# One row in place of a broadcast load, and a pool closed in two steps: a transformer block on one core

## The chip, the cores and the metric

The kernel runs on one core of one Trainium2 chip. The core has five engines with queues of their own: TensorE (PE, matrix products), VectorE (DVE), ScalarE (ACT), GpSimd (POOL) and SyncE (SP), which here only issues the DMAs. Each engine takes its instructions strictly in the order in which the program has written them; engines wait for each other by semaphores. The metric is the device time of one execution in microseconds.

## The reference

One layer on 1024 tokens of width 1024, all in float32: a half-weighted SwiGLU feed-forward block, a mixing block with three kinds of attention, and a second feed-forward block like the first.

```python
def rms_norm(x, g):
    x32 = x.astype(jnp.float32)
    y = x32 * lax.rsqrt(jnp.mean(x32 * x32, axis=-1, keepdims=True) + EPS) * g.astype(jnp.float32)
    return y.astype(x.dtype)

def swiglu(h, w_in, w_out):
    gate, up = jnp.split(h @ w_in, 2, axis=-1)
    return (jax.nn.silu(gate) * up) @ w_out
...
    x = x + 0.5 * swiglu(rms_norm(x, ffn1_norm), ffn1_w_in, ffn1_w_out)
...
    x = x + mix @ w_mix_out
    x = x + 0.5 * swiglu(rms_norm(x, ffn2_norm), ffn2_w_in, ffn2_w_out)
```

D_FF is 2816, so `w_in` is 1024x5632 and `w_out` 2816x1024. `mix` is the sliding-window attention with sinks beside a gated sum of compressed, selected and windowed attention; the change doesn't touch it.

## The kernel before

**Numbers.** Every float32 operand of a product is split into a high part (`whi`, `gph`, names ending in h), which ACT or POOL makes by a copy, and a low part (`wlo`, `gpl`, names ending in l), which DVE makes by a subtraction. A product is three matmuls, high by high, high by low, low by high (`mm3`, lines 250 to 252).

**Stages.** A feed-forward block has two stages. The first (`first_stage`) computes gate and up. `X` (eight tiles x0 to x7 of 128 tokens) is normalised and flipped by PE transposes (`ntr`, line 312) into operands `A11`, `A12` (in `XN0`) and `A21`, `A22`, from which come further sums `S1` to `S4`. Columns n of `w_in` are then worked in groups of seven products, in which combinations of blocks stand for the eight of plain block multiplication; the last three products of a group take S3, S4 and A22 in this order (in the code m7, m3, m4). The results go to DRAM (`AS`). The second stage (`second_stage`) reads them back as `graw`, splits them into `gph` and `gpl`, and multiplies them with `w_out` (`wraw`, `whi`, `wlo`): steps k = 0 to 10 for each of seven products, twelve matmuls a step. The second block does the same with other names of pools.

**Pools.** The operands A21/S4 (one place for both), A22, S2, S1, S3 of the first stage lie in one pool `p_in` (line 573); at its end the pool is closed, and the second stage's pool `p_out` with `graw`, `gph`, `gpl` is opened over its place (`to_out`, `to_out2`). The kernel waits tile by tile for the users of the memory that a new tile lies over. Between the two, `p_xn` takes the place of S4 and A22 for the normalised rows of the next block.

**Order.** The order of every engine's instructions is made when the program is built. `Plan.run` keeps a list of tasks, each with an engine, a cost, a position, tasks that it depends on (`deps`), tasks that must have been written earlier (`after`) and slots of rings; it simulates the engines and writes the task that could begin first, by position among those that are near. So a task that becomes free earlier in the plan moves ahead in its engine's queue, and it holds whatever is behind it. The task `opened` carries `to_out`, and all second-stage loads have it in `after`:

```python
    opened = add(None, 0.0, at - 5.0, to_out, after=chain_[-1:])
```

`chain_` is the last seven products of the first stage, so `chain_[-1]` is m4 and `chain_[4]` is m7. A load of `graw` also depends on m6 (`chain_[2]`), its split on m7.

**Beginning.** `load_x` brings x0, `load_gain` the norm's vector with one DMA that reads the same 4 KB for each of the 128 partitions (512 KB arrive), then x1 and eight weight tiles of 256 KB (`wraw`) in turn with x2 to x7. `inv_rms` squares a tile in two halves on ACT (lines 500, 506), and finishes the reciprocal root in small DVE instructions (lines 473 to 476, 503, 509). `scale_in_place` (line 520) multiplies the tile with root and gain on DVE. POOL and DVE split the weights (lines 457, 460). PE fills its time with transposes of the identity (`warm`). `wraw` has four slots.

Of the kernel before, what the change touches and what calls it, by code (L numbers as in the profile page):

```python
# [8 lines left out]
F32 = mybir.dt.float32  # L9
F32R = mybir.dt.float32r  # L10
BF16 = mybir.dt.bfloat16
I32 = mybir.dt.int32
AF = mybir.ActivationFunctionType
# [8 lines left out]
KD = 8  # L22
# [35 lines left out]
class Units:  # L58
# [7 lines left out]
    def add(self, width, parts):  # L66
        self.units.append((width, parts))
        return len(self.units) - 1
# [120 lines left out]
def block_kernel(  # L189
# [26 lines left out]
    PE, ACT, DVE, POOL = nc.tensor, nc.scalar, nc.vector, nc.gpsimd  # L216
    ctx.enter_context(tc.manual_schedule())

    def pool(name, stack=None, **kw):
        return (stack or ctx).enter_context(tc.tile_pool(name=name, bufs=1, reuse_waits="tile", **kw))  # L220
# [84 lines left out]
    def load_gain(dst, g):  # L305
        dma(dst, dram_ap(g, 0, [[0, 128], [1, D]]))
# [17 lines left out]
    def xn_tiles(p):  # L324
        return [XA, [p.tile([128, KD, 512], F32R, name="xn1" + s) for s in "hl"]]
# [193 lines left out]
    def scale_in_place(t, r, gain, pos, deps):  # L519
        return add("D", 1.22, pos, lambda: DVE.scalar_tensor_tensor(  # L520
            X[t], X[t], r(), gain(), op0=OP.mult, op1=OP.mult), deps=deps)
# [39 lines left out]
    HALF = [slice(0, 512), slice(512, 1024)]  # L561
# [8 lines left out]
    def in_src(w_in, n, j, part):  # L570
        return dram_ap(w_in, 512 * j * 2 * FF + part * FF + n * 128, [[4 * 2 * FF, 128], [2 * FF, 4], [1, 128]])

    def open_in(p):

        t = {k: [p.tile([128, 4, 512], F32R, name=k + s) for s in "hl"] for k in ("S4", "A22", "S2", "S1", "S3")}
        t["A21"] = t["S4"]
        t["A11"], t["A12"] = XN0
        return t
# [357 lines left out]
    ph1 = ExitStack()  # L936
    nws = ExitStack()
    f_in = ExitStack()
    p_nw = pool("p_nwf", f_in, side="right")
    opn1 = open_in(pool("p_in", f_in))  # L940
    gain1 = p_nw.tile([128, D], F32, name="gain1")
    extra = [p_nw.tile([128, 512], F32, name="ext%d" % j) for j in range(2)]
    r_y = Ring("hr", [128, 4, 8], F32, 6)
    new_plan([])

    load_x(0, n=2)
    come = lambda at: add(None, 0.0, 0.0, lambda: None, tail=at)
    xt, raws1 = [[come(3.3), come(4.05)]] + [None] * 7, {}
    fetched[-1] = come(0.75)
    fetched.append(add("S", 1.46, -20.0, lambda: load_gain(gain1, ffn1_norm), after=fetched[-1:], tail=2.2))  # L950
    for w_ in (1, (0, 0, 0), (0, 0, 1), 2, (0, 1, 0), (0, 1, 1), 3, (1, 0, 0), (1, 0, 1), 4, (1, 1, 0), (1, 1, 1), 5, 6, 7):
        if type(w_) is tuple:
            raws1[w_] = fetch(in_src(ffn1_w_in, *w_), -20.0)
        else:
            fetched.append(add("S", 1.46, -20.0, lambda t=w_: load_x(t, n=2 if t < 4 else 1), after=fetched[-1:], tail=2.2))
            xt[w_] = [fetched[-1]]
    w_ = add(None, 0.0, 0.0, lambda: None, tail=1.4)
    for j in range(WARM):
        w_ = add("P", 0.64, 9.0, lambda: warm_up(3), deps=[w_], takes=[(r_mo, [])])
    scaled = {}  # L960
    for t in range(NT):
        p_ = 1.0 * t if t < 4 else 8.0 + 1.0 * t
        st, d, yu = inv_rms(t, p_, xt[t] if t == 0 else xt[t] * 2, True)
        scaled[t] = scale_in_place(t, lambda st=st: st["y"], lambda: gain1, p_, [d])
        yu.append(scaled[t])
    at, chain_, stored_, gone = first_stage(0, ffn1_w_in, ffn1_w_out, lambda: opn1, scaled, lambda: extra,
                                         lambda: [gain1[:, h] for h in HALF], 2.0, "G", [], 
                                              [(0, 256), (256, 512)], none, raws=raws1)

    def to_out():  # L970
        nonlocal p_nw, xn, p_o
        f_in.close()
        xn = xn_tiles(pool("p_xn", ph1))
        p_o = pool("p_out", f_out)
        p_nw = pool("p_nw", nws, side="right")
        mem["gain"] = p_nw.tile([128, D], F32, name="gainm")

    def parameters():
        load_gain(mem["gain"], mix_norm)
        for key, qn_, kn_ in (("a", q_norm_a, k_norm_a), ("b", q_norm_b, k_norm_b)):  # L980
# [1 line left out]
            gk[key] = p_o.tile([128, HD], F32, name="gk" + key)  # L982
            dma(gq[key], dram_ap(qn_, 0, [[0, 128], [1, HD]]))
            dma(gk[key], dram_ap(kn_, 0, [[0, 128], [1, HD]]))
    xn = p_o = None
    gq, gk = {}, {}
    f_out = ExitStack()
    opened = add(None, 0.0, at - 5.0, to_out, after=chain_[-1:])
    asked = add("S", 2.4, at + 14.0, parameters, deps=[add(None, 0.0, at, lambda: None, after=[opened], deps=chain_[-1:], tail=8.0)])
    r_nx = Slots(2)  # L990
    again = {t: [add("S", 1.46, at - 4.0 + t, lambda t=t: load_x(t), deps=gone, after=[opened], tail=2.2)]
             for t in range(NT)}
# [6 lines left out]
    at = second_stage(0, ffn1_w_out, at, opened, (chain_[2], chain_[4]), stored_, lambda: p_o, again, each)  # L999
# [963 lines left out]
        scaled[t] = scale_in_place(t, lambda t=t: R2[:, t:t + 1], lambda: nx["t"][:, 0, :D], p_, [put_, r_, gain2])  # L1963


    f_in, f_out = ExitStack(), ExitStack()
    opn2 = {"A11": XN0[0], "A12": XN0[1]}
    extra2 = []

    def to_ffn2():  # L1970
        att.close()
        kvs.close()
        opn2.update(open_in(pool("p_in2", f_in)))
        p = pool("p_nw2", f_in, side="right")
        extra2.extend(p.tile([128, 512], F32, name="ext2%d" % j) for j in range(4))
    settled = add(None, 0.0, tail + 10.0, to_ffn2, deps=attention, after=list(scaled.values()))
# [2 lines left out]

    def to_out2():  # L1980
        nonlocal p_o
        f_in.close()
        p_o = pool("p_out2", f_out)
    opened2 = add(None, 0.0, at - 5.0, to_out2, after=chain_[-1:])
    again = {t: [add("S", 1.46, at - 4.0 + t, lambda t=t: dma(X[t], XS[t]), deps=gone, after=[opened2], tail=2.2)]
             for t in range(NT)}
    xout = out.rearrange("b (t p) d -> (b t) p d", p=128)
# [3 lines left out]
    second_stage(1, ffn2_w_out, at, opened2, (chain_[2], chain_[4]), stored_, lambda: p_o, again, each2)  # L1991
    plan.run()
    f_out.close()


_INS = ['x', 'rel_bias_table', 'ffn1_norm', 'ffn1_w_in', 'ffn1_w_out', 'mix_norm', 'w_mix_in', 'w_mix_out',
# [26 lines left out]
```

## Time and profile before

| | us |
|---|---|
| median of 3 runs | 1943.32 |
| lowest, highest | 1943.04, 1943.46 |
| the profiled execution, its own time | 1940.19 |
| its span, first to last instruction | 1938.4 |
| PE busy in the span | 1892.4 (98%) |
| DVE, ACT, POOL busy | 1365.0, 917.4, 404.8 |

In the rows below the first number is a start in microseconds from the start of the span, the second a duration; "<-" stands between what an instruction writes and what it reads, xN for N instructions alike, and in brackets stands how long the engine had been idle before, and what ended that. Matmuls overlap, so the distance of two starts is their pace.

### The profile page before, as it was taken

The page shows a single profiled execution, that of the slowest core. Times are in us where ns is not written, and L with a number is a line of the kernel's source. Part 1 is how long each engine was busy: PE and PEld are TensorE (multiplying, and loading weights), DVE is VectorE, ACT ScalarE, POOL GpSimd, SP SyncE. Part 2 cuts the span into 40 slices and gives each one's busy share as a digit, 9 for nine tenths or more (in the row PEclk, how much of TensorE's full clock was granted, in tenths as well). Part 3 has the DMA queues.
Part 4 walks back from the last instruction along what each step waited for, and adds up shares of the span by engine and source line. Part 5 has one row for each costly group of instructions (what it writes and reads, how often), then busy time and mean ns, then how long its engine had stood idle before and what let it go on. Part 6 is the DMA issues. An engine that isn't in the chain of part 4 may idle for free.

```text
span 1938.4 us, 28044 instructions
## 1 busy us (share of the span) xinstructions
PE 1892.4 (98%) x9142; PEld 1580.0 (82%) x9142; DVE 1365.0 (70%) x3114; ACT 917.4 (47%) x1947; POOL 404.8 (21%) x544
## 2 busy tenths in 40 slices
PE   7999999999999999998899999989999999999999
PEld 6888888887888888887788788778888888878887
DVE  7687876665655677566888888876978766655553
ACT  5343333333444434245877888843433333344442
POOL 3011111111000112013754765530111111110000
PEclk9999999999999999998999999999999999999999
DMA  5277753336886337235202321022777533368662
GB/s 174 76 241 242 234 190 104 97 121 212 296 274 196 115 88 195 71 119 168 67 12 58 102 72 56 23 76 70 243 243 234 189 103 98 120 223 296 198 217 98
DMA packets 243955, 291.29 MB, mean 150 GB/s; under 512 B 24912, under 2 KB 138976, under 8 KB 243808
## 3 DMA queue, kind: packets, MB, share of 16 engines
q1 hardware_dynamic: 243808, 289.50, 46.3%
q8 instruction: 72, 1.18, 0.3%
q14 instruction: 75, 0.61, 0.1%
HBM read 202.24 MB, written 90.33 MB: 151 GB/s over the span
## 4 chain that ended last, share of the span: by engine, by line
PE 92%; DVE 3%; ACT 2%; POOL 1%; DMA 1%; issue 1%; SPq 0%; DVEq 0%; ACTq 0%; POOLq 0%
PE lg L250 13%; PE lg L252 13%; PE lg L251 13%; PE mo L250 6%; PE mo L252 6%; PE mo L251 6%; PE pv L250 4%; PE pv L252 4%; PE pv L251 4%; PE ptr L1825 3%; PE a L252 3%; PE a L251 3%; PE a L250 3%; PE pvo L1845 2%; PE pvo L1844 2%; PE lg L1650 2%
## 5 line engine op out<-in xcount | busy, mean ns | idle before, releaser
L801 POOL TENSOR_TENSOR x<-x,x 128x512 f32<-128x512 f32 x80 | 115.2, 1439 | 710.5 <-DVE x L797 670.0
L460 DVE TENSOR_TENSOR wlo<-wraw,whi 128x512 fp32r<-128x512 f32 x290 | 203.8, 708 | 74.9 <-ACT whi L455 70.8
L455 ACT ACTIVATE whi<-wraw 128x512 fp32r<-128x512 f32 x274 | 170.1, 623 | 111.3 <-PE lg L251 43.6
L460 DVE TENSOR_TENSOR gpl<-graw,gph 128x512 fp32r<-128x512 f32 x154 | 105.1, 689 | 142.7 <-ACT gph L455 142.6
L455 ACT ACTIVATE gph<-graw 128x512 fp32r<-128x512 f32 x154 | 96.1, 630 | 187.8 <-PE pv L251 84.7
L793 ACT ACTIVATE x<-lg 128x512 f32<-128x512 f32 x96 | 57.4, 598 | 157.7 <-PE lg L252 157.7
L1835 DVE TENSOR_TENSOR pl<-ptr,ph 128x512 fp32r<-128x512 f32 x178 | 116.5, 685 | 16.8 <-ACT ph L1833 15.5
L1833 ACT ACTIVATE ph<-ptr 128x512 fp32r<-128x512 f32 x178 | 98.7, 595 | 33.2 <-PE ptr L1825 31.8
L250 PE MATMUL a<-whi,gph 128*128 128x512 f32 x264 | 104.1, 394 | 3.6 <-ACT gph L455 3.6
L252 PE MATMUL a<-whi,gpl 128*128 128x512 f32 x264 | 104.0, 394 | 1.4 <-DVE gpl L460 1.4
L251 PE MATMUL a<-wlo,gph 128*128 128x512 f32 x264 | 103.6, 392 | 0.0
L88 POOL TENSOR_SCALAR whi<-wraw 128x512 fp32r<-128x512 f32 (+1 forms) x52 | 35.4, 685 | 325.3 <-PE mo L252 221.2
L250 PE MATMUL lg<-xn0h,whi 128*128 128x512 f32 (+1 forms) x264 | 100.5, 381 | 0.0
L251 PE MATMUL lg<-xn0l,whi 128*128 128x512 f32 (+1 forms) x264 | 99.9, 378 | 0.2 <-DVE xn0l L320 0.2
L252 PE MATMUL lg<-xn0h,wlo 128*128 128x512 f32 (+1 forms) x264 | 99.8, 378 | 0.0
L455 ACT ACTIVATE whi<-x 128x512 fp32r<-128x512 f32 x104 | 64.9, 628 | 72.5 <-PE lg L251 35.9
L460 DVE TENSOR_TENSOR wlo<-x,whi 128x512 fp32r<-128x512 f32 x104 | 71.2, 686 | 29.8 <-ACT whi L455 29.8
L797 DVE TENSOR_TENSOR x<-lg,x 128x512 f32<-128x512 f32 x72 | 49.7, 690 | 53.1 <-PE lg L252 52.8
L250 PE MATMUL lg<-whi,gph 128*128 128x512 f32 x198 | 77.0, 389 | 0.0
L251 PE MATMUL lg<-wlo,gph 128*128 128x512 f32 x198 | 77.0, 389 | 0.0
L252 PE MATMUL lg<-whi,gpl 128*128 128x512 f32 x198 | 77.0, 389 | 0.0
L250 PEld LDWEIGHTS a<-whi,gph 128*128 128x128 f32 x264 | 50.2, 190 | 14.6 <-ACT gph L455 4.4
(481 smaller groups left out, 5685.6 us busy)
## 6 DMA issues: line engine op xcount, KB each, us to landing
wraw<-in_ffn_w_in_dram SPq DMA_DIRECT2D x176, 256.0 KB, 3.4
wraw<-in_ffn_w_out_dram SPq DMA_DIRECT2D x66, 256.0 KB, 3.0
x<-in_ffn_w_out_dram SPq DMA_DIRECT2D x44, 256.0 KB, 3.8
qd<-qst SPq DMA_DIRECT2D x32, 256.0 KB, 2.3
xn0l<-qd SPq DMA_DIRECT2D x32, 256.0 KB, 2.7
wraw<-in_w_mix_in_dram SPq DMA_DIRECT2D x28, 256.0 KB, 2.9
x<-in_x_dram SPq DMA_DIRECT2D x12, 512.0 KB, 8.3
gain<-in_ffn_w_out_dram SPq DMA_DIRECT2D x22, 256.0 KB, 4.9
```

The costliest lines, as they stand in the source:

```text
L250: PE.matmul(o, ah, bh, start=first, stop=False, **kw)
L251: PE.matmul(o, ah, bl, start=False, stop=False, **kw)
L252: PE.matmul(o, al, bh, start=False, stop=last, **kw)
L455: ACT.activation(w["h"], b["r"], AF.Copy)
L460: low = add("D", 0.69, pos + 0.5, lambda: DVE.tensor_tensor(w["l"], b["r"], w["h"].bitcast(F32), op=OP.subtract), deps=chain[-1:])
L793: ACT.activation(b["r"], o["o"], act)
L797: return add("D", 0.69, at, lambda b=tb[k], o=bx[o]: DVE.tensor_tensor(b["r"], o["o"], b["r"], op=OP.add), deps=deps)
L801: return add("G", 1.25, at, lambda a=tb[a], b=tb[b]: POOL.tensor_tensor(a["r"], a["r"], b["r"], op=OP.mult), deps=deps)
L1650: PE.matmul(o, s.Q[:, h], ks[:, c0 + c:c0 + c + m], start=True, stop=False, skip_group_check=True)
L1825: PE.transpose(p[:, h * 128:(h + 1) * 128], s.P[h][:, c:c + 128], ident)
L1833: ACT.activation(st["ph"], st["p"], AF.Copy)
L1835: lo = add("D", 0.6, pos + 0.2, lambda st=st: DVE.tensor_tensor(st["pl"], st["p"], st["ph"].bitcast(F32), op=OP.subtract), deps=[hi])
```

## The change

The norm's vector comes as two rows of 512 elements on one partition (into the first row of the scratch tiles ext0, ext1), and PE multiplies each with a column of ones, which spreads it over 128 partitions; ACT copies the two results into `gain1`. The scaling of all x tiles depends on both copies. The operands S4/A21 and A22 move into the place of `xn[1]`, which is opened from the start (in the second block into a pool `p_xn2`); the pool of S2, S1, S3 (`f_op`) is closed after m7 in the written order, and the scratch on the right side (`f_in`) after m4 and the users of its tiles.

```diff
-    def open_in(p):
-        t = {k: [p.tile([128, 4, 512], F32R, name=k + s) for s in "hl"] for k in ("S4", "A22", "S2", "S1", "S3")}
+    def open_in(p, x):
+        t = {k: [p.tile([128, 4, 512], F32R, name=k + s) for s in "hl"] for k in ("S2", "S1", "S3")}
+        t["S4"], t["A22"] = ([v[:, 4 * a:4 * a + 4] for a in range(2)] for v in x)
         t["A21"] = t["S4"]
...
-    opn1 = open_in(pool("p_in", f_in))
+    xn = xn_tiles(pool("p_xn", ph1))
+    f_op = ExitStack()
+    opn1 = open_in(pool("p_in", f_op), xn[1])
...
+    ones = p_nw.tile([1, 128], F32, name="ones")
+    DVE.memset(ones, 1.0)
...
+    for h in range(2):
+        dma(extra[h][:1], dram_ap(ffn1_norm, h * 512, [[512, 1], [1, 512]]))
     fetched[-1] = come(0.75)
-    fetched.append(add("S", 1.46, -20.0, lambda: load_gain(gain1, ffn1_norm), after=fetched[-1:], tail=2.2))
...
+            PE.matmul(box["o"], ones, extra[h][:1], start=True, stop=True)
+        t = add("P", 1.7, -1.0, rows_of_gain, deps=[come(3.4)], takes=[(r_lg, us)])
+        spread.append(add("A", 0.6, -1.0, lambda h=h, box=box: ACT.activation(gain1[:, HALF[h]], box["o"], AF.Copy),
+                          deps=[t]))
...
-        scaled[t] = scale_in_place(t, lambda st=st: st["y"], lambda: gain1, p_, [d])
+        scaled[t] = scale_in_place(t, lambda st=st: st["y"], lambda: gain1, p_, [d, *spread])
...
     def to_out():
-        nonlocal p_nw, xn, p_o
+        nonlocal p_o
+        f_op.close()
+        p_o = pool("p_out", f_out)
+
+    def to_norm():
+        nonlocal p_nw
         f_in.close()
-        xn = xn_tiles(pool("p_xn", ph1))
-        p_o = pool("p_out", f_out)
         p_nw = pool("p_nw", nws, side="right")
...
-    opened = add(None, 0.0, at - 5.0, to_out, after=chain_[-1:])
+    opened = add(None, 0.0, at - 8.0, to_out, after=chain_[4:5])
+    normed = add(None, 0.0, at, to_norm, after=chain_[-1:] + gone)
...
-    opened2 = add(None, 0.0, at - 5.0, to_out2, after=chain_[-1:])
+    opened2 = add(None, 0.0, at - 8.0, to_out2, after=chain_[4:5])
```

What this makes of the written order shows at two places. The first is ACT where the first feed-forward block passes from stage one to stage two. `x1<-pv` and the last `x6<-lg` are copies of products out of PSUM (the last one is m4's), `whi` are weights of the second stage, `gph` its read-back operands. Before:

```order
L793 ACTIVATE x1_75<-pv_4042 128x512
L455 ACTIVATE whi_4075<-wraw_4000 128x512
L455 ACTIVATE whi_4094<-wraw_4020 128x512
L455 ACTIVATE whi_4129<-wraw_4040 128x512
L793 ACTIVATE x6_80<-lg_3981 128x512
L455 ACTIVATE whi_4142<-wraw_4060 128x512
L455 ACTIVATE gph_4148<-graw_4126 128x512
L455 ACTIVATE gph_4154<-graw_4132 128x512
```

The four `whi` here are the weights of steps 5 to 8, and both `gph` stand behind the copy of m4's result. The same place now:

```order
L794 ACTIVATE x1_75<-pv_4052 128x512
L455 ACTIVATE whi_4091<-wraw_4010 128x512
L455 ACTIVATE whi_4114<-wraw_4030 128x512
L455 ACTIVATE gph_4122<-graw_4089 128x512
L455 ACTIVATE gph_4127<-graw_4094 128x512
L455 ACTIVATE whi_4143<-wraw_4050 128x512
L455 ACTIVATE gph_4152<-graw_4097 128x512
L794 ACTIVATE x6_80<-lg_3991 128x512
```

The two `whi` ahead of the `gph` are those of steps 5 and 6; the first three `gph` have moved ahead of the copy of m4's result, and the first two ahead of the weight of step 7. On SP the loads of the weights of steps 9 and 10 have moved from ahead of the first read-backs to behind them. The second place is DVE at the beginning of the program, from the first scaling on (the `hr` rows are the small instructions of a root; hr_420 belongs to x0, hr_441 to x1). Before:

```order
L520 SCALAR_TENSOR_TENSOR x0_74<-x0_74,hr_420,gain1_398 128x1024
L460 TENSOR_TENSOR wlo_455<-wraw_414,whi_454 128x512
L460 TENSOR_TENSOR wlo_466<-wraw_422,whi_465 128x512
...
L460 TENSOR_TENSOR wlo_490<-wraw_448,whi_489 128x512
L460 TENSOR_TENSOR wlo_502<-wraw_458,whi_501 128x512
L520 SCALAR_TENSOR_TENSOR x1_75<-x1_75,hr_441,gain1_398 128x1024
```

Here x0 is scaled ahead of all low parts, x1 behind those of the first four weight tiles. Now, with hr_457 and hr_499 of x2 and x3:

```order
L460 TENSOR_TENSOR wlo_473<-wraw_435,whi_472 128x512
L460 TENSOR_TENSOR wlo_486<-wraw_442,whi_485 128x512
L520 SCALAR_TENSOR_TENSOR x0_74<-x0_74,hr_428,gain1_399 128x1024
L520 SCALAR_TENSOR_TENSOR x1_75<-x1_75,hr_432,gain1_399 128x1024
L503 TENSOR_SCALAR hr_457<-hr_457 128x1
...
L520 SCALAR_TENSOR_TENSOR x2_76<-x2_76,hr_457,gain1_399 128x1024
L473 RECIPROCAL hr_499<-hr_499 128x1
...
L320 TENSOR_TENSOR xn0l_90<-ntr_531,xn0h_89 128x4x128
```

Both scalings now stand behind the low parts of the third and fourth weight tiles, and the low part of x1's first flip (ntr_531) stands behind the scaling of x2 and the root of x3.

## Rows read from the trace of the kernel before

**Rows 1.** The page's busy times of the engines, in the span: engine, busy microseconds, share, count.

```profile
PE 1892.4 (98%) x9142; PEld 1580.0 (82%) x9142; DVE 1365.0 (70%) x3114; ACT 917.4 (47%) x1947; POOL 404.8 (21%) x544
```

**Rows 2.** The waits of PE over the whole span: who waited for what; microseconds in total, times, the longest.

```profile
PE ntr L312 <- DVE x L520: 6.5, 3, 4.4
...
PE a L250 <- ACT gph L455: 3.6, 2, 1.8
...
PE a L252 <- DVE gpl L460: 1.4, 2, 0.7
```

**Rows 3.** The chain of waits at the beginning of the span, in order of time: start, duration, what.

```profile
1.63 6.04 DMA gain<-in_ffn_norm_dram
...
7.70 6.31 DMA wraw<-in_ffn_w_in_dram
...
14.08 1.05 POOL whi L457
...
15.76 1.29 DVE x L520
...
17.09 2.00 PE ntr L312 x8
...
20.39 1.95 PE ntr L312 x8
```

**Rows 4.** The DMA issue of the first half of x0, first of all; engine, count, KB, microseconds from issue to landing.

```profile
x<-in_x_dram SPq DMA_DIRECT2D x1, 256.0 KB, 2.9
```

**Rows 5.** The timeline of ACT and DVE at the beginning.

```profile
8.42 0.63 ACT L500 ACTIVATE junk<-x 128x512 bf16<-128x512 f32 x1 [2.82 <-DMA x<-in_x_dram]
8.96 0.19 ACT L500 ACTIVATION_READ_ACCUMULATOR junk<-x 128x1 f32 x1
10.12 0.29 ACT L506 ACTIVATE hr<-hr 128x1 f32<-128x1 f32 x1
12.21 1.13 ACT L316 ACTIVATE xn0h<-ntr 128x512 fp32r<-128x512 f32 x2
15.15 0.69 DVE L460 TENSOR_TENSOR wlo<-wraw,whi 128x512 fp32r<-128x512 f32 x1 [0.51 <-POOL whi L457]
19.01 1.27 DVE L520 SCALAR_TENSOR_TENSOR x<-x,hr,gain 128x1024 f32<-128x1024 f32 x1
33.14 2.48 DVE L520 SCALAR_TENSOR_TENSOR x<-x,hr,gain 128x1024 f32<-128x1024 f32 x2
```

**Rows 6.** The timeline of PE where the first products begin.

```profile
21.99 0.56 PE L250 MATMUL lg<-xn0h,whi 128*128 128x256 f32 x1
22.35 0.41 PE L251 MATMUL lg<-xn0l,whi 128*128 128x256 f32 x1
22.56 0.41 PE L252 MATMUL lg<-xn0h,wlo 128*128 128x256 f32 x1
...
24.24 0.28 PE L251 MATMUL lg<-xn0l,whi 128*128 128x256 f32 x1
24.36 0.28 PE L252 MATMUL lg<-xn0h,wlo 128*128 128x256 f32 x1
```

**Rows 7.** The timeline of PE at the passage of the first block.

```profile
461.60 0.39 PE L251 MATMUL lg<-A22l,whi 128*128 128x512 f32 x1
461.83 0.39 PE L252 MATMUL lg<-A22h,wlo 128*128 128x512 f32 x1
464.00 0.50 PE L250 MATMUL a<-whi,gph 128*128 128x512 f32 x1 [1.78 <-ACT gph L455]
...
465.46 0.80 PE L252 MATMUL a<-whi,gpl 128*128 128x512 f32 x1 [0.65 <-DVE gpl L460]
466.05 0.63 PE L250 MATMUL a<-whi,gph 128*128 128x512 f32 x1
466.48 0.63 PE L251 MATMUL a<-wlo,gph 128*128 128x512 f32 x1
...
471.93 0.40 PE L250 MATMUL a<-whi,gph 128*128 128x512 f32 x1
```

**Rows 8.** The timeline of ACT at the same place.

```profile
456.63 0.63 ACT L455 ACTIVATE whi<-wraw 128x512 fp32r<-128x512 f32 x1 [1.43 <-issue]
459.36 0.63 ACT L455 ACTIVATE whi<-wraw 128x512 fp32r<-128x512 f32 x1 [2.09 <-PE pv L251]
462.31 0.60 ACT L793 ACTIVATE x<-lg 128x512 f32<-128x512 f32 x1 [2.32 <-PE lg L252]
...
463.32 2.18 ACT L455 ACTIVATE gph<-graw 128x512 fp32r<-128x512 f32 x4
```

**Rows 9.** DMA issues of SP at the same place, from the timeline (start, duration), and of the first read-back its time to landing.

```profile
453.30 0.33 SPq L257 DMA_DIRECT2D wraw<-in_ffn_w_out_dram  x1
455.96 0.33 SPq L257 DMA_DIRECT2D wraw<-in_ffn_w_out_dram  x1
458.13 0.33 SPq L257 DMA_DIRECT2D wraw<-in_ffn_w_out_dram  x1
458.51 0.42 SPq L257 DMA_DIRECT2D graw<-as_0A  x1
...
graw<-as_0A SPq DMA_DIRECT2D x1, 256.0 KB, 3.7
```

**Rows 10.** Stretches around both passages: stretch, its length, then busy time and count of PE, PEld, DVE, ACT, POOL; the granted clock of PE, the busy share of the DMA engines, GB/s.

```profile
464.00:471.20 7.20, 6.55 (x16) 4.83 (x17) 4.50 (x7) 2.57 (x6) 0.60 (x2) 0.53 0.91 304
1722.00:1730.00 8.00, 5.48 (x24) 4.19 (x24) 4.86 (x7) 5.10 (x9) 1.27 (x1) 1.00 0.94 328
```

**Rows 11.** The timeline of PE at the passage of the second block.

```profile
1721.68 0.39 PE L252 MATMUL lg<-A22h,wlo 128*128 128x512 f32 x1
1723.86 0.50 PE L250 MATMUL a<-whi,gph 128*128 128x512 f32 x1 [1.78 <-ACT gph L455]
...
1725.32 0.50 PE L252 MATMUL a<-whi,gpl 128*128 128x512 f32 x1 [0.73 <-DVE gpl L460]
...
1725.89 0.39 PE L251 MATMUL a<-wlo,gph 128*128 128x512 f32 x1
```

More of the change, by code (lines that the diff above doesn't have):

```diff
@@ L956, in block_kernel, with rows_of_gain @@
             xt[w_] = [fetched[-1]]
+    spread = []
+    for h in range(2):
+        box, us = {}, []
+        def rows_of_gain(h=h, box=box):
+            box["o"] = bank("lg")
+            PE.matmul(box["o"], ones, extra[h][:1], start=True, stop=True)
+        t = add("P", 1.7, -1.0, rows_of_gain, deps=[come(3.4)], takes=[(r_lg, us)])
+        spread.append(add("A", 0.6, -1.0, lambda h=h, box=box: ACT.activation(gain1[:, HALF[h]], box["o"], AF.Copy),
+                          deps=[t]))
+        us.append(spread[-1])
     w_ = add(None, 0.0, 0.0, lambda: None, tail=1.4)
@@ L984, in parameters @@
             dma(gk[key], dram_ap(kn_, 0, [[0, 128], [1, HD]]))
-    xn = p_o = None
+    p_o = None
     gq, gk = {}, {}
     f_out = ExitStack()
-    opened = add(None, 0.0, at - 5.0, to_out, after=chain_[-1:])
-    asked = add("S", 2.4, at + 14.0, parameters, deps=[add(None, 0.0, at, lambda: None, after=[opened], deps=chain_[-1:], tail=8.0)])
+    opened = add(None, 0.0, at - 8.0, to_out, after=chain_[4:5])
+    normed = add(None, 0.0, at, to_norm, after=chain_[-1:] + gone)
+    asked = add("S", 2.4, at + 14.0, parameters, deps=[add(None, 0.0, at, lambda: None, after=[normed], deps=chain_[-1:], tail=8.0)])
     r_nx = Slots(2)
@@ L1963, in block_kernel @@
         scaled[t] = scale_in_place(t, lambda t=t: R2[:, t:t + 1], lambda: nx["t"][:, 0, :D], p_, [put_, r_, gain2])
-    f_in, f_out = ExitStack(), ExitStack()
+    f_in, f_op, f_out = ExitStack(), ExitStack(), ExitStack()
     opn2 = {"A11": XN0[0], "A12": XN0[1]}
@@ L1972, in to_ffn2 @@
         kvs.close()
-        opn2.update(open_in(pool("p_in2", f_in)))
+        x = pool("p_xn2", f_in)
+        x = [x.tile([128, KD, 512], F32R, name="xn2" + s) for s in "hl"]
+        opn2.update(open_in(pool("p_in2", f_op), x))
         p = pool("p_nw2", f_in, side="right")
@@ L1981, in to_out2 @@
         nonlocal p_o
-        f_in.close()
+        f_op.close()
         p_o = pool("p_out2", f_out)
-    opened2 = add(None, 0.0, at - 5.0, to_out2, after=chain_[-1:])
+    opened2 = add(None, 0.0, at - 8.0, to_out2, after=chain_[4:5])
     again = {t: [add("S", 1.46, at - 4.0 + t, lambda t=t: dma(X[t], XS[t]), deps=gone, after=[opened2], tail=2.2)]
@@ L1993, in block_kernel @@
     f_out.close()
+    f_in.close()
 _INS = ['x', 'rel_bias_table', 'ffn1_norm', 'ffn1_w_in', 'ffn1_w_out', 'mix_norm', 'w_mix_in', 'w_mix_out',
```

## The prediction

> **What bounds the kernel now.** I read the busy times first: PE works in 98% of the span [rows 1], so the end moves only by what PE waits for, or by its pace. Then the waits of PE [rows 2]: three groups touch the change. Flips wait 6.5 us for the scaling of x, at the beginning; the first matmuls of the second stage wait 3.6 us for `gph` and 1.4 us for `gpl`, in two times each, once per feed-forward block. Third the chain at the beginning [rows 3]: the gain's DMA, the weight tiles behind it, POOL's and DVE's split of the fourth weight tile, the scaling of x1, the flips of x1 and of x2, then the first product at 21.99 us [rows 6]. Last the timelines at the two passages [rows 7 to 11]. The median of the runs, 1943.32, lies 3.1 us above the profiled execution's own time, 1940.19 (whose span is 1938.4); I take all differences from the profiled one and subtract them from the median.
>
> **The passage of the first block.** In rows 7 PE's pace at full clock is 0.23 us a matmul (461.60 to 461.83; the average over a step of twelve, which the code's planner also uses, is 0.2275). m4's last matmul starts at 461.83. The matmul at 471.93 is the 19th after it, counted in the same timeline. Without a wait it would start at 461.83 + 19 x 0.2275 = 466.15. So the passage costs 471.93 - 466.15 = 5.8 us: 1.78 + 0.65 us of waiting, and the rest slow matmuls, whose starts lie 0.43 us apart (466.05 to 466.48), twice the pace. The granted clock in that stretch is 0.53 of full [rows 10], that is the 1.2 GHz level for nearly all of it; PE had just waited 1.78 us and again 0.65 us.
>
> Does the change remove it? What held the first `gph` is rows 8: ACT could take it only at 463.32, because ahead of it in the queue stood the copy of m4's result, which starts at 462.31 when m4 is done, and one weight. The read-back itself was issued at 458.51 and landed 3.7 us later, at 462.2 [rows 9]; the load alone would have let `gph` start a microsecond earlier. Both move. In the new order of SP the last two weight loads of rows 9 stand behind the first read-back, so it goes out behind the load of 453.30, at 453.6 (m6, whose operand lay in its place, ends four products of 2.73 us ahead of m4, at 451.1), and lands by 457.3 with the same 3.7 us. In the new order of ACT `gph` 0 and 1 stand behind the weight of step 6, which starts at 456.63 (it waits for a slot that m7 frees), and ahead of everything that waits for m3 or m4: 456.63 + 0.63 = 457.3, then two at 0.55 each (2.18 for four, rows 8): 457.9 and 458.4. DVE takes the low part of that weight until 458.0 and `gpl` 0 until 458.7 (0.69 each, as in rows 5). PE wants `gph` at 462.06 and `gpl` two matmuls later at 462.5: spare 4.2 and 3.8 us. What is late next is `gph` 2, now behind the weight of step 7 that waits for m3 (459.36): 460.5, wanted two steps later at 467.5; and `gph` 3 behind m4's copy, 463.4, wanted at 470.2. So the pause goes, and with it the half clock: -5.8 us. If the read-back came later by more than the 3.8 us, each further microsecond would come back one to one.
>
> **The passage of the second block.** The same order, the same pause (1.78 + 0.73), but here the clock stays full [rows 10, 11]. The fifth matmul behind m4's last starts at 1725.89 in place of 1721.68 + 5 x 0.2275 = 1722.82: 3.1 us. -3.1 us, by the same walk. [...]
>
> **The beginning.** Removed: a DMA that lands 6.0 us after its issue at 1.63, with all behind it [rows 3]. x1's first half then starts on ACT at 8.42 [rows 5]. Now two rows of 2 KB are issued in its place (0.43 each, a timing of any SP issue, as the 0.42 in rows 9), so x1 is issued at 2.5 and lands by the 2.9 us of x0's half [rows 4] at 5.4: 3.0 us earlier. The loads behind were packed, so the fourth weight tile, whose POOL copy began at 14.08 [rows 3], begins at 11.1. Added on PE, ACT and DVE: a memset, two products, two copies. A product of a one-row float32 operand is not in the trace. Its bounds: one pass of 512 columns at half clock, 0.43 us [rows 7], and 1.7 us, the cost in the change's own task; I take 1.7, the worse. Rows land by about 5, both products end by 8.4, and the second copy, behind two halves of x1 and one of x2 on ACT, ends near 10.3. Nothing needs it before DVE reaches the first scaling: the fourth weight tile's copy ends at 11.1 + 1.05 = 12.1, its low part at 12.8, and the new order has both scalings behind it. Spare 2.5 us: these products cost nothing.
>
> Where do the 3.0 us go? The scalings run 12.8 to 15.3 (2.48 for two, rows 5), so x1 is ready 1.75 us earlier than in rows 3, but x0 is late: 14.0, where it was done before 11. PE then flips x0 and x1 in one go, 14.1 to 18.0 (2.0 each, rows 3), and ACT takes x0's high parts until 16.7. Behind these stand in ACT's queue the second squares of x2 and x3, 0.8 each, and their roots, 0.3 each: until 18.9. DVE's root of x2 (0.75) and the check-in of x3 (0.2) follow, x2 is scaled 19.6 to 20.8, where it was 19.01 to 20.28 [rows 5]. x2's second flip needs a PSUM bank that DVE frees with the low part of x1's first flip, which now stands behind x2's scaling and x3's root: 20.8 + 0.75 + 0.7 = 22.2. Flip until 23.1 at worst, against 21.99 before; I walked the old order the same way and came out 0.4 late, so I take 22.6: +0.6 us. The clock also matters: at the start matmuls of 256 columns lie 0.21 apart, after about ten of them 0.12 [rows 6]. If the rise came 30 matmuls later, 30 x 0.09 = 2.7 us would be lost; if the order cost nothing, the 3.0 us would stay. So this term lies between -3.0 and +3.3, taken as +0.6, nearest to the walk.
>
> Everything later shifts with PE. The parameters' loads and the reload of x stand elsewhere in SP's queue in the second stage, beside 190 us of PE work with no wait on them; cost nothing.
>
> Sum: 1943.3 - 5.8 - 3.1 + 0.6 = 1935.0 us.
>
> **The rivals.**
> First, both passages lose their pause and the beginning keeps its 3 us: 1943.3 - 8.9 - 3.0 = 1931.4. For it: all loads are earlier. Against it: DVE's order, above.
> Second, the timed runs fall to half clock at the second passage too, as the profiled one did at the first [rows 10]. Then 2.7 us more come back (5.8 - 3.1): 1932.3. [...] For it: the median is 3.1 us above the profiled execution, which this would explain. Against it: rows 10.
> Third, the beginning loses 3.3 us by a later rise of the clock: 1937.7.
> Fourth, half of it: ACT's copy or the read-back comes late and a pause remains at both passages, say 1.5 us of 2.4, with the clock falling at the first: 1943.3 - 0.9 - 0.9 + 0.6 = 1942.1, no change that can be told (below).
> Fifth, on the other side: the read-backs wait for m4 although they are written earlier, because the place in memory is released with it. They would be issued at 462.1, land 3.7 later at 465.8, and `gph`, which stands on ACT ahead of m4's copy, would end at 466.4 where it ended at 463.9: +2.5 us at each passage, and the clock would then fall at the second one too (+2.7): 1943.3 + 2.5 + 2.5 + 2.7 + 0.6 = 1951.6. It decides as soon as the first read-back is issued behind 457.8 (462.1 less 3.7 and 0.6). Against it: already before, SP issued the read-back at 458.51, while m3 ran [rows 9]; its tile lies over S2, not over A22.
>
> **How the numbers follow.** About 0.2% or 3.9 us is what a measurement of this kernel can tell from no change: below 1939.4 is faster, above 1947.2 slower. Forecast (1933.5 to 1936.5): 0.5. First rival 0.1, second 0.15, third 0.12: with the forecast 0.87 for faster. Fourth 0.09: same. Fifth 0.04: slower. The range 1931 to 1939.5 holds the forecast and the first three, and leaves out the last two.
>
> **What the changed profile would show.** Right: no wait of PE for `gph` or `gpl` at the passages, the first read-back issued some 8 us ahead of m4's end, `gph` 0 some 4 us ahead of it on ACT; granted clock 1.00 there; x1's first square near 5.4, its scaling about 13 to 15, the first product between 22 and 23.5. Wrong: a row "PE a <- ACT gph" of over 1 us, a first product behind 25 or ahead of 20.5, or new stretches at half clock elsewhere, which would move the time by microseconds for no step of this walk.

## The result and the profile after

The changed kernel takes 1932.05 us in the median of 4 runs (1931.91 to 1932.16), the kernel before 1943.18 beside it (4 runs, 1940.82 to 1943.46): ratio 0.9949, 95% interval 0.9937 to 0.996. So it is faster by 11.1 us in the medians, 7.8 to 12.2 us by the interval; 1935.0 was predicted, with a range from 1931 to 1939.5. The profiled execution of the changed kernel is one of 1931.91 us with a span of 1930.1. From profile to profile the difference is 1940.19 - 1931.91 = 8.3 us, which is the sum of the prediction and lies inside that interval; where the other 2.8 us are from, if they are more than scatter, is a question for the runs.

The waits of PE after, whole span (microseconds in total, times, the longest), the counterpart of [rows 2]:

```profile
PE ntr L312 <- DVE x L520: 3.6, 2, 3.3
...
PE ntr L312 <- issue: 2.9, 1, 2.9
...
PE ntr L312 <- DVE xn0l L320: 1.8, 2, 1.6
```

The rows for `gph` and `gpl` are gone: 5.0 us of waiting less. The flips wait 3.6 us for the scaling in place of 6.5, and 2.9 us behind an issue that the profile doesn't explain further, where that was 1.3.

The timeline of PE at the first passage after (start, duration; compare [rows 7]). m4's operand A22 now bears the name of the tile that it lies in, xn1:

```profile
462.43 0.39 PE L251 MATMUL lg<-xn1l,whi 128*128 128x512 f32 x1
462.65 0.39 PE L252 MATMUL lg<-xn1l,wlo 128*128 128x512 f32 x1
462.88 0.39 PE L250 MATMUL a<-whi,gph 128*128 128x512 f32 x1
463.11 0.39 PE L251 MATMUL a<-wlo,gph 128*128 128x512 f32 x1
463.33 0.39 PE L252 MATMUL a<-whi,gpl 128*128 128x512 f32 x1
```

The seam can't be told from the matmuls around it: 0.23 us from each start to the next. What stands behind this on SP and ACT, to be read against [rows 8, 9]; first SP's issues, then ACT:

```profile
454.55 0.38 SPq L257 DMA_DIRECT2D graw<-as_0A  x1
454.98 0.42 SPq L257 DMA_DIRECT2D graw<-as_1A  x1
...
456.93 2.37 SPq L257 DMA_DIRECT2D wraw<-in_ffn_w_out_dram  x2
```

```profile
457.46 0.63 ACT L455 ACTIVATE whi<-wraw 128x512 fp32r<-128x512 f32 x1 [1.43 <-issue]
458.08 1.31 ACT L455 ACTIVATE gph<-graw 128x512 fp32r<-128x512 f32 x2
460.18 0.63 ACT L455 ACTIVATE whi<-wraw 128x512 fp32r<-128x512 f32 x1 [0.79 <-PE pv L251]
460.72 0.61 ACT L455 ACTIVATE gph<-graw 128x512 fp32r<-128x512 f32 x1
463.14 0.60 ACT L794 ACTIVATE x<-lg 128x512 f32<-128x512 f32 x1 [1.80 <-PE lg L252]
463.63 1.14 ACT L455 ACTIVATE gph<-graw 128x512 fp32r<-128x512 f32 x2
```

The first read-back goes out 8.1 us ahead of m4's last matmul, and the first two `gph` begin 5.1 us ahead of the copy of m4's result (463.14), which they stood behind before. Both passages in windows (columns as in [rows 10]): 41 matmuls in 9.10 us, full clock, no gap.

```profile
462.60:471.70 9.10, 9.10 (x41) 7.53 (x41) 8.39 (x13) 5.40 (x10) 1.84 (x3) 1.00 0.92 299
1716.50:1725.60 9.10, 9.10 (x41) 7.51 (x41) 8.14 (x13) 5.42 (x10) 1.47 (x2) 1.00 0.93 306
```

At the beginning, the timelines of PE, ACT, POOL and DVE after, to be read against [rows 3, 5, 6]:

```profile
4.13 3.78 PE L969 MATMUL lg<-ext,ones 1*128 1x512 f32 x4
...
15.85 3.50 PE L312 MATMUL ntr<-ident,x 128*128 128x128 f32 x16 [3.27 <-DVE x L520]
22.22 1.01 PE L312 MATMUL ntr<-ident,x 128*128 128x128 f32 x4 [2.87 <-issue]
23.43 1.13 PE L312 MATMUL ntr<-ident,x 128*128 128x128 f32 x4 [0.20 <-DVE xn0l L320]
24.21 0.56 PE L250 MATMUL lg<-xn0h,whi 128*128 128x256 f32 x1
```

```profile
6.22 0.63 ACT L500 ACTIVATE junk<-x 128x512 bf16<-128x512 f32 x1 [1.90 <-DMA x<-in_x_dram]
...
10.95 0.58 ACT L971 ACTIVATE gain<-lg 128x512 f32<-128x512 f32 x1
```

```profile
12.86 1.02 POOL L457 TENSOR_SCALAR whi<-wraw 128x512 fp32r<-128x512 f32 x1 [0.27 <-DMA wraw<-in_ffn_w_in_dram]
```

```profile
13.91 0.69 DVE L460 TENSOR_TENSOR wlo<-wraw,whi 128x512 fp32r<-128x512 f32 x1 [0.51 <-POOL whi L457]
14.52 2.83 DVE L520 SCALAR_TENSOR_TENSOR x<-x,hr,gain 128x1024 f32<-128x1024 f32 x2
...
20.84 1.28 DVE L520 SCALAR_TENSOR_TENSOR x<-x,hr,gain 128x1024 f32<-128x1024 f32 x1
...
22.69 0.68 DVE L320 TENSOR_TENSOR xn0l<-ntr,xn0h 128x512 fp32r<-128x512 f32 x1
```

The second copy of the gain is done at 11.53, three microseconds ahead of the scalings, which stand behind the low part of the fourth weight tile (13.91). The first product starts at 24.21 where it was 21.99. By m4 of the first passage only 0.8 us of these 2.2 are left (462.65 against 461.83).

### The profile page after: what moved, and what is told of

The parts are those of the page before. It is cut to its first block, busy times and chain, and to the rows that moved or that the text cites. A ratio compares the mean times of both kernels' runs of the same rounds, so it can differ in the third digit from the quotient of the medians.

```text
span 1930.1 us, 28079 instructions
## 1 busy us (share of the span) xinstructions
PE 1891.4 (98%) x9146; PEld 1578.6 (82%) x9146; DVE 1366.9 (71%) x3115; ACT 917.2 (48%) x1949; POOL 407.1 (21%) x544
## 4 chain that ended last, share of the span: by engine, by line
PE 92%; DVE 3%; ACT 2%; POOL 2%; DMA 1%; issue 1%; SPq 0%; POOLq 0%; DVEq 0%; ACTq 0%
PE lg L250 13%; PE lg L251 13%; PE lg L252 13%; PE mo L250 6%; PE mo L252 6%; PE mo L251 6%; PE pv L250 4%; PE pv L252 4%; PE pv L251 4%; PE ptr L1846 3%; PE a L251 3%; PE a L250 3%; PE a L252 3%; PE pvo L1866 2%; PE pvo L1865 2%; PE lg L1671 2%
## 5 line engine op out<-in xcount | busy, mean ns | idle before, releaser
L1734 POOL TENSOR_SCALAR Psel<-Psel,sc,gates 128x256 f32<-128x256 f32 (+7 forms) x60 | 52.3, 875 | 45.6 <-DVE sc L1726 19.3
```

What stands on the lines that cost most here:

```text
L1734: POOL.tensor_scalar(P[:, off:e], P[:, off:e], sc, gate, op0=OP.mult, op1=OP.mult)
```

## The experiments

Below, "loss" at a passage is worked out for every profiled execution in the same way: start of the 40th matmul behind m4's last one, less that one's start, less 40 x 0.2275 us. In the changed kernel it is 0.0 at both; in the profile of before 5.8 and 3.0. These two, less the 0.8 us by which the changed kernel comes to the first passage later, make 8.0 of the 8.3 us between the two profiles: the stretch between the passages (1254.1 and 1253.9 us without the losses) and the one behind the second (213.7 and 213.6) hardly differ.

**The pool split alone.**

```diff
...
-    for h in range(2):
-        dma(extra[h][:1], dram_ap(ffn1_norm, h * 512, [[512, 1], [1, 512]]))
     fetched[-1] = come(0.75)
+    fetched.append(add("S", 1.46, -20.0, lambda: load_gain(gain1, ffn1_norm), after=fetched[-1:], tail=2.2))
...
-        scaled[t] = scale_in_place(t, lambda st=st: st["y"], lambda: gain1, p_, [d, *spread])
+        scaled[t] = scale_in_place(t, lambda st=st: st["y"], lambda: gain1, p_, [d])
```

> Only the second part of the change: the pool split and the earlier written read-backs; the gain comes by the old broadcast load and the scalings do not wait for copies. Theory (the passages are the whole gain, the row costs about 0.8 us by the time of the first passage): both pauses gone, first product of the first block again near 22.0 us, so 0.4 to 0.8 us below the changed kernel, 1931.2 to 1931.7 us. Rival (the row at the beginning gives something): above the changed kernel's 1932.05, up to 1935.

Measured: 1933.16 us (1931.69 to 1934.18), ratio to the kernel before 0.9953, interval 0.994 to 0.9965. Loss at both passages 0.0. The whole gain that can be told is in this part: the ratio is that of the full change when it was measured again (below). The theory's range is missed by 1.5 us, and the median lies in the rival's. That the row gives something is not shown by it all the same: the five runs spread over 2.5 us, and m4's last matmul of the first passage starts at 463.67 here, no earlier than with the row (462.65), though the first product does (22.85 against 24.21).

**The row alone.** The kernel before with the other half of the diff (rows, products, copies).

> Only the first part of the change: the gain as one row, spread by products with ones; pools and the order of the second stage as before. Theory: both pauses stay (a wait for gph of about 1.8 us in each block), the beginning costs 0.4 to 0.8 us: 1943.6 to 1944.0 us. Rival (earlier loads help): 1940 to 1942.5 us, with the first product no later than 22.0.

Measured: 1942.84 us (1939.1 to 1944.64), ratio 1.0002, interval 0.9993 to 1.0011: no difference that can be told, and a median between the two ranges. The waits for `gph` are there, 1.78 us each, losses 4.7 and 3.1. The first product starts at 24.20, so the rival's condition isn't met either.

**The written order as before, the memory as changed.**

```diff
-    opened = add(None, 0.0, at - 8.0, to_out, after=chain_[4:5])
+    opened = add(None, 0.0, at - 5.0, to_out, after=chain_[-1:])
...
-    opened2 = add(None, 0.0, at - 8.0, to_out2, after=chain_[4:5])
+    opened2 = add(None, 0.0, at - 5.0, to_out2, after=chain_[-1:])
```

> The changed kernel with the two opening tasks written behind m4 again, as before; the places in memory stay as the change has them. Theory (the place in the written order makes the pause, memory alone does not take it away): the order of ACT at the first passage is that of before, both pauses return at 1.7 to 1.9 us with the fall of the clock, 1943 to 1944.5 us. Rival (what held the read-backs was that their memory was released with m4's operand): no pause, 1931.5 to 1932.5 us.

Measured: 1941.71 us (1941.19 to 1945.04), 1.3 us under the range expected, ratio 1.0003, interval 0.9994 to 1.0012. The pauses are those of before, 1.78 and 0.73 us. The windows behind them, in the profiled execution of 1943.47 us:

```profile
465.20:472.20 7.00, 6.25 (x19) 4.69 (x20) 4.98 (x8) 3.16 (x6) 0.62 (x2) 0.76 0.91 303
1725.60:1732.60 7.00, 6.27 (x19) 4.71 (x20) 4.68 (x8) 2.86 (x6) 0.25 (x1) 0.76 0.94 310
```

The clock fell at both passages, for less of the stretch than in [rows 10]; losses 4.7 and 4.7. So the split of the memory alone gives nothing that can be told; what counts is where the loads and splits stand in the written order. The other half, the early order without the split, wasn't tried: A22 would lie in a pool that is already closed.

**The kernel before again.**

> The kernel before, unchanged, to get another profiled execution of it. Theory (the executions at 1943 have the half clock behind the pause of the second block too, the one at 1940.2 had it behind the first alone): a profiled execution of about 1943 shows a granted clock near 0.5 for some 7 us at both passages, and one of 1940 to 1941 shows it at one of them. Rival: an execution of 1943 shows the second passage at full clock, and the 2.7 us lie elsewhere.

Measured: 1941.74 us (1936.49 to 1943.07); the profiled execution, 1941.29 us, has losses of 3.0 and 4.5. The windows behind its two pauses:

```profile
464.79:472.00 7.21, 6.47 (x27) 5.09 (x28) 6.48 (x11) 3.58 (x7) 0.61 (x2) 1.00 0.83 265
1723.52:1730.00 6.48, 5.75 (x18) 4.35 (x19) 4.50 (x7) 2.75 (x5) 0.26 (x1) 0.74 0.97 330
```

The pauses are the same to the hundredth (1.78 and 0.73 us), but here the clock falls at the second passage and not at the first, the reverse of [rows 10], and for about half of the 7 us that the theory asked for. In the number of falls the theory holds: one in this execution of 1941.3 and in that of 1940.2, and two in the one of 1943.5 above, whose passages are written alike. But the passages don't make the difference in time. They cost 8.8 us in the execution of 1940.2, 7.5 in that of 1941.3 and 9.3 in that of 1943.5. The rest lies elsewhere: m4's last matmul of the first passage starts at 461.8, 462.6 and 463.0, and the stretch between the passages takes 1254.1, 1255.7 and 1255.7 us without their losses. In the two longer executions the clock also falls in that stretch, here from 1274.0 to 1277.5 us, where the profile of before has full clock. That a run of 1943 of the kernel before itself has two falls at its passages, no profile has shown.

The loss is 3.0 us without a fall, 4.5 to 5.8 with one, and which it is changes from execution to execution of one kernel. Over the eight passages with the full pause that were profiled (two each of the kernel before, of it again, of the row alone and of the order as before) the mean is (5.79+3.04+3.04+4.46+4.67+3.05+4.67+4.66) / 8 = 4.2 us.

**The changed kernel again.**

> The changed kernel, unchanged, beside more executions of the kernel before. Theory (the kernel before loses 2.5 us at each passage always and a further 0, 1.7 or 3.4 us to the half clock, by execution; the changed one loses nothing there): 1931.7 to 1934 us, and a spread at least as narrow as that of the pool split alone, 2.5 us, against the 7 us of the kernel before. Rival (the few executions of the changed kernel so far were lucky): some at 1936 us or above.

Measured: 1932.02 us (1931.21 to 1932.86) against 1941.38 for the kernel before in 18 runs beside it, which go from 1937.04 to 1944.34. Ratio 0.9953, interval 0.994 to 0.9967, or 9.1 us. Nine runs of the changed kernel in all lie within 1.7 us of each other.

**Loads early, splits behind m4.**

```diff
-    at = second_stage(0, ffn1_w_out, at, opened, (chain_[2], chain_[4]), stored_, lambda: p_o, again, each)
+    at = second_stage(0, ffn1_w_out, at, opened, (chain_[2], chain_[-1]), stored_, lambda: p_o, again, each)
```

and the same in the second block.

> The changed kernel, but the splits of the first eight read-backs stand behind m4 in the plan; the loads stay early. Theory (ACT's order makes the pause: gph behind the copy of m4's result): loads land some 5 us before they are used, and PE still waits 1.1 to 1.4 us for gph (1.78 less the one weight of 0.5 us that no longer stands between), 0.7 for gpl, at both passages: 1.9 us each and the clock on top, 1936 to 1940 us. Rival (it was the time of the loads): no wait, 1932 to 1934 us.

Measured: 1940.26 us (1938.68 to 1941.93), 8.2 above the changed kernel beside it, a little over the range expected. Against the kernel before the ratio is 0.9993 (interval 0.9984 to 1.0003): early loads alone give nothing that can be told. The wait is there. First ACT, then PE at the first passage:

```profile
463.36 0.60 ACT L794 ACTIVATE x<-lg 128x512 f32<-128x512 f32 x1 [2.33 <-PE lg L252]
463.85 2.70 ACT L455 ACTIVATE gph<-graw 128x512 fp32r<-128x512 f32 x5
```

```profile
464.53 0.50 PE L250 MATMUL a<-whi,gph 128*128 128x512 f32 x1 [1.26 <-ACT gph L455]
465.92 0.50 PE L252 MATMUL a<-whi,gpl 128*128 128x512 f32 x1 [0.66 <-DVE gpl L460]
```

The read-back was issued at 454.77 here, and still `gph` begins only behind the copy of m4's result. ACT's order makes the pause, not the load; the 1.26 us are the 1.78 less the one weight (0.5) that is no longer between. This execution has no fall at a passage (loss 2.5 each, 4.9 in both), but one in the middle of the program, which the two profiles of the changed kernel don't have there: granted clock 0.50 from 760.7 to 764.1, worth some 1.7 us. That accounts for this execution (1939.0 us), not for the median; what its other executions lost is not recorded.

**Read-backs behind m4**, as late as the fifth rival of the prediction has them: `(chain_[-1], chain_[4])` in the same place.

> The changed kernel, but the first eight read-backs stand behind m4 in the plan (the fifth rival of the prediction, made on purpose). Theory: issued at about 462.5 us at the first passage, landed near 466, PE waits 3.5 to 4.5 us for gph in each block, with the fall of the clock behind it: 1943 to 1949 us. Rival (the loads come early enough even so): a wait under 2 us, 1937 to 1942 us.

Measured: 1946.99 us (1944.93 to 1948.49), ratio 1.003, interval 1.0019 to 1.004. The read-back goes out at 463.44, `gph` waits for it on ACT, and PE waits 3.97 and 4.28 us; losses 7.1 and 6.7, with a fall of the clock at both passages. SP, ACT and PE at the first:

```profile
463.44 0.42 SPq L257 DMA_DIRECT2D graw<-as_0A  x1
466.57 1.94 ACT L455 ACTIVATE gph<-graw 128x512 fp32r<-128x512 f32 x3 [2.08 <-DMA graw<-as_0A]
467.25 0.79 PE L250 MATMUL a<-whi,gph 128*128 128x512 f32 x1 [3.97 <-ACT gph L455]
```

A late load can thus cost more than a late place on ACT; in the kernel before it merely wasn't the last to come.

**Filling the pause.** The kernel before with seven matmuls behind m4 in each block, whose result nobody uses:

```diff
+    def fill():
+        o = bank("a", name="fill")
+        xh = opn1["A11"][0]
+        for i in range(7):
+            PE.matmul(o, xh[:, 0, :128], xh[:, 1, :], start=i == 0, stop=i == 6, skip_group_check=True)
+    add("P", 1.6, at, fill, after=chain_[-1:], takes=[(r_a, [])])
```

> The kernel before with seven matmuls of 512 columns, on operands that lie there anyway, written between m4 and the first matmul of the second stage in both blocks; their result is used by nobody. They take some 1.6 us of PE inside the pause, which stays. Theory (the idle time of PE brings the clock down, in some executions): the wait for gph falls from 1.78 to about 0.2 us, stage two starts when it did, no stretch at half clock at either passage; the four profiled executions with the full pause so far had 5.1 us at half clock there on average, so 2.5 us less than the kernel before, ratio 0.9987. Rival (the clock falls there for another reason, or the 0.7 us of waiting for gpl are enough): stretches at half clock remain, ratio 1.000.

Measured: 1939.43 us (1938.15 to 1941.52) against 1941.63 (1939.46 to 1943.26), ratio 0.9992, interval 0.9983 to 1.0. PE at the first passage, then the windows of both:

```profile
461.95 1.75 PE L974 MATMUL fill<-xn0h 128*128 128x512 f32 x7
463.89 0.50 PE L250 MATMUL a<-whi,gph 128*128 128x512 f32 x1 [0.20 <-ACT gph L455]
```

```profile
461.90:469.00 7.10, 6.16 (x26) 4.45 (x26) 4.46 (x7) 4.22 (x8) 1.63 (x2) 1.00 0.96 307
1720.40:1727.50 7.10, 6.16 (x26) 4.46 (x26) 4.03 (x6) 4.20 (x8) 1.28 (x1) 1.00 0.89 314
```

Full clock at both, losses 3.1 and 3.1 (the seven matmuls left out of the count), the price of a pause without a fall. This is what the theory of the idle engine asks for. The other profiles go with it: in the seven without a pause (the changed kernel twice, the pool split alone, and the four runs below) none of the 14 passages shows a fall, of the two with 1.26 us (the splits behind m4) none does, of the eight with the full pause five do, and of the two with the pause of about 4 us above both. Whether the filling itself kept the clock up isn't settled: three of eight passages with the full pause kept it too, so that two of two do so by chance about one time in seven, and the interval of the time reaches to 1.0.

**The products done twice**, into the same place.

> The changed kernel with each product of the gain with ones done twice, into the same place. Theory (these products cost nothing, since the scalings wait for DVE's order): products last 7.5 us in place of 3.78, end near 11.6, the first copy of the gain is 1.9 us later, and the scaling of x0 starts no more than 0.7 us later than 14.52. Rival (the products are on the path): scaling of x0 at 17 to 18 us.

PE and DVE there:

```profile
4.13 2.07 PE L969 MATMUL lg<-ext,ones 1*128 1x512 f32 x2
6.00 1.91 PE L970 MATMUL lg<-ext,ones 1*128 1x512 f32 x2
7.70 1.91 PE L969 MATMUL lg<-ext,ones 1*128 1x512 f32 x2
9.41 1.91 PE L970 MATMUL lg<-ext,ones 1*128 1x512 f32 x2
```

```profile
12.60 1.71 DVE L460 TENSOR_TENSOR wlo<-wraw,whi 128x512 fp32r<-128x512 f32 x2
14.23 2.82 DVE L520 SCALAR_TENSOR_TENSOR x<-x,hr,gain 128x1024 f32<-128x1024 f32 x2
```

The scalings begin at 14.23, no later than 14.52: the products cost nothing there. The expectation had the first copy 1.9 us later; it came at 8.43 (8.36 without), since ACT took the squares of x1 and x2 until then, which the expectation had left out. The one run took 1934.91 us, 2 us more than any run of the changed kernel. Its trace does not put that on the products: m4's last matmul of the first passage starts at 462.79 (462.65 and 463.38 in the two profiles of the changed kernel), and it is between the passages that 2.9 to 3.2 us more go by; in that stretch the clock falls from 756.9 to 760.3, as it does in neither of those two.

**The order at the beginning mended.** The changed kernel with the low parts of the third and fourth weight tiles behind the scalings of x0 and x1 on DVE, and the gain's second copy ahead of the first square of x2 on ACT:

```diff
...
-        low = add("D", 0.69, pos + 0.5, lambda: DVE.tensor_tensor(w["l"], b["r"], w["h"].bitcast(F32), op=OP.subtract),
-                  deps=chain[-1:])
+        low = add("D", 0.69, pos + 0.5, lambda: DVE.tensor_tensor(w["l"], b["r"], w["h"].bitcast(F32), op=OP.subtract),
+                  deps=chain[-1:], after=list(behind))
...
+                                          behind=[scaled[0], scaled[1]] if raws and n == 0 and j == 1 else [])
...
+        if t == 2:
+            xt[t] = [add(None, 0.0, 0.0, lambda: None, deps=[xt[t][0], spread[1]]), xt[t][0]]
```

> The changed kernel with DVE's and ACT's order at the beginning mended: the low parts of the third and fourth weight tiles stand behind the scalings of x0 and x1, and the second copy of the gain ahead of the first square of x2. Theory (the order on DVE holds the scalings, not the row): scaling of x0 at 9.7 to 11.5 us where it began at 14.52, first product 2 to 5 us ahead of 24.2, time 1 to 4 us below the changed kernel's run beside it. Rival (the loads of x2 and x3 and the later start of the clock decide): first product earlier, but the same time within 1 us.

Measured: 1930.05 us (1928.76 to 1930.74) against 1932.02 (1931.21 to 1932.86) of the changed kernel beside it: 2.0 us, five runs each that don't overlap. PE, then DVE:

```profile
18.45 1.13 PE L312 MATMUL ntr<-ident,x 128*128 128x128 f32 x4 [1.05 <-DVE xn0l L320]
19.23 0.56 PE L250 MATMUL lg<-xn0h,whi 128*128 128x256 f32 x1
```

```profile
10.29 0.69 DVE L460 TENSOR_TENSOR wlo<-wraw,whi 128x512 fp32r<-128x512 f32 x1 [1.26 <-POOL whi L457]
...
12.90 2.79 DVE L520 SCALAR_TENSOR_TENSOR x<-x,hr,gain 128x1024 f32<-128x1024 f32 x2
```

The first product comes 5.0 us earlier, as expected, though the scaling came at 12.90 and not by 11.5: the low part of the second weight tile (10.29) and both roots still stand ahead of it. Which of the two moves, on DVE or on ACT, gave how much was not tried.

**One step further**, that tile's low part behind the scalings too, beside the mended order once more.

> The mended order one step further: the low part of the second weight tile, too, stands behind the scalings of x0 and x1. Theory (each thing that stands ahead of the scalings on DVE delays the first product): scaling of x0 at 9.9 to 10.5 us where it was 12.90, first product 16.5 to 18 us where it was 19.23, 1 to 2.5 us less time than the mended order beside it. Rival (x2, x3 and the weights bound the stretch behind it): same time within 1 us.

> The mended order again, for comparison on the same chip: 1929 to 1931 us, 2 us under the changed kernel.

Measured: 1929.66 us (1928.52 to 1930.35) beside 1930.41 (1927.27 to 1930.51). The scaling came at 10.93, the first product at 17.62, but the times can't be told apart: the rival held. Against the kernel before, 1941.63, the ratios are 0.994 and 0.9941 (intervals 0.9927 to 0.9954 and 0.9928 to 0.9953). So the mended order beats both kernels of this case, and the further step adds nothing that can be told.

## Why the prediction came out as it did

**First passage, -5.8: right**, for its execution and step by step. The walk had the read-back go out at 453.6, `gph` 0 begin at 457.3 and `gph` 2 end at 460.5; with all 0.8 us later these came at 454.55, 458.08 and 461.33. The run with the splits behind m4 showed that the order on ACT was the right place to look. As a figure for the median the 5.8 are the highest of eight losses.

**Second passage, -3.1: right** for its execution, and low as a figure for the median, which may hold a fall there too.

**The step that failed** is "I take all differences from the profiled one and subtract them from the median". The profiled execution lost 5.8 + 3.1 = 8.9 at the passages; what the runs at 1943 lost there was another number. Eight passages give 2 x 4.2 = 8.4 us a run on average, and in three larger sets (60 runs, 1937.04 to 1945.35) the median of the kernel before is 1941.4 to 1941.8. From there the sum of -8.3 says 1933.1 to 1933.5; the first three runs lay in the upper part of that spread. With the changed kernel beside one of these sets the difference was 9.1 us (interval 6.4 to 11.6), which holds the sum. As it stands, the 1932.05 lies inside the range and below the 1933.5 to 1936.5 that the prediction gave half its chances.

**The second rival**, a fall at the second passage in the timed runs, priced at 2.7 us more, gave 1932.3 and came nearest to the 1932.05. Two of four profiles with the full pause show a fall there, at a loss of 4.5 and 4.7, not 5.8. But that the number came near is no sign that the mechanism did: the profiled execution with a fall at both passages lost 9.3 us there, only 0.5 more than the 8.8 of the profile of before, and the stretch between the passages varies by 2.6 us over the four profiles (1253.2 to 1255.7). The timed runs leave no rows, so what makes the 2.8 us stays open.

**The clock behind the pause.** Of eight passages with the same pause of 1.78 us five show a fall and three none. The Trainium skill ("TensorE: Matmul & The Clock Gate", section "HAM oscillation — how this bites in real kernels") tells of a kernel whose clock fell behind each wait for data; those waits were longer than the 1.78 us here, so the Trainium skill doesn't say there what this pause does. The measurement says: a fall, but not each time.

**The beginning, +0.6: right as a sum by luck, wrong in its steps.** m4's last matmul of the first passage starts at 461.83, 462.62, 463.67 and 461.72 in four profiles with the broadcast load, and at 462.65, 463.38, 462.83, 463.04, 462.87 and 462.89 in six with the row as the change has it: 0.5 us later on average, inside a scatter of 1 to 2 us. The step that failed is "3.0 us earlier" for the loads. x1's first square began at 6.22 where it was 8.42, 2.2 us earlier, and the fourth weight tile's copy at 12.86 where it was 14.08, 1.2 earlier. I had x1 land within the 2.9 us that x0's first half took, which went out first of all; x1's loads go out at 2.29 now, beside others, and the first square begins 3.9 us later. And I had passed the same 3.0 us on to all loads behind. Nearer is an estimate from the bytes that went away: 512 KB at the 257 to 340 GB/s that the DMA engines moved then (4 to 8 us and 8 to 12 us of the profile of before) are 1.5 to 2 us. So the scalings came at 14.5, not 12.8. That x2's second flip waits for a bank, freed by the low part of x1's first flip, was right; that low part ended at 23.37 (22.69 and 0.68), 1.2 us later than the walk's 22.2, and the first product came at 24.2, not 22.6 and not by the 23.1 of the worst case.

So at the first product the change was 2.2 us late and not 0.6. Of these, 1.4 us came back until m4, by steps that the walk doesn't have: 0.8 are a wait of a flip for A22l, which the profile of before has and that of after hasn't; the rest was not followed up. The third rival didn't come: the clock rose after eight matmuls of the first products in place of ten.

**That the gain's products cost nothing: right**, even done twice. The product's price had the bounds 0.43 and 1.7 us; 7.70 - 6.00 = 1.7 is measured.

**The fifth rival's price**, 2.5 us more waiting at each passage, can be read from the read-backs behind m4. For `gph` alone it was about right: 3.97 - 1.78 = 2.2 and 4.28 - 1.78 = 2.5. But the wait for `gpl` went away there, so that all the waiting grew by 1.5 and 1.8 us, and the time was 5.6 us above the kernel before, where the rival had 8.3 (1951.6 - 1943.3).

## What to carry to other kernels

Where a stage ends and the next begins, look at what stands ahead of the first operand's preparation in its engine's queue: here it stood behind the copy of the old stage's last product, which has to wait for that product, and behind one weight of 0.5 us; that cost 3 to 6 us at each seam, and early loads alone did not help. A loss that hangs on the clock is not the same in two executions of one kernel, so take such a term from several profiles, or give it a range. And what the removed load freed here, 1.2 to 2.2 us, was nearer to its bytes over the rate at which the queue moved (1.5 to 2 us) than to its time to landing (6.0).

## What the runs showed of the hardware

In one execution of one kernel (the kernel before again) the same pause of PE, 1.78 and 0.73 us, was followed by a granted clock of 1.00 at the first passage and of 0.74 at the second. Without a pause no passage of 14 shows a fall. The clock also falls where no passage is, in every profile near 900 us (904.8 to 915.1 in that of before), and in some near 1275 us but not in others of the same kernel. A float32 product of one row with 128 columns of ones, 512 wide, is recorded as two matmuls and takes 1.7 us at the beginning of the program, where 15 identity transposes behind it take 4.74, or 0.32 each.
